# A hybrid SSD and convolution layer: another hand-written issue order for PE, DVE, ACT and POOL

## The chip, the core and the metric

The kernel runs on one core of one Trainium2 chip. The metric is the device time of one launch in microseconds (us); lower is better. The engines are named as in the profile: PE (TensorE, matmul), PEld (its weight load), DVE (VectorE), ACT (ScalarE), POOL (GpSimd), SP (SyncE, which issues all DMAs here). Each runs its own stream of instructions in order and waits on semaphores where it needs another engine's result.

## The reference, cut to what matters

One trunk layer is applied to 128 context tokens and 512 latent tokens, width 1024. All of it is float32.

```python
mod = silu(cond) @ w_ada + b_ada                # 6 shifts, scales and gates
h = rms_norm(x, norm_mix_pre) * (1 + sc1) + sh1
z, xbc, dt_raw, cf_in = split(h @ w_in)
xbc = silu(dwconv1d(xbc, w_ssd_conv))           # width 3
...
y_f, s_f = ssd_chunked(xs, dt_f, a_f, b_mat, c_mat, init_f)
y_b, s_b = ssd_chunked(flipped ...)             # 16 heads, chunks of 128 tokens
y_ssd = rms_norm((y_f + flip(y_b) + xs * d_skip) * silu(z), ssd_norm)
cf_a, cf_g = split(cf_in)
u = dwconv1d(cf_a * sigmoid(cf_g), w_cf_conv)   # width 31
u = silu(layer_norm(u))
x = x + g1 * rms_norm(concat(y_ssd, u) @ w_out, norm_mix_post)
h = rms_norm(x, norm_ffn_pre) * (1 + sc2) + sh2
up = dwconv2d(h @ w_ffn_up, w_ffn_conv)         # 3x3 on the latent grid, width 3 on context
x = x + g2 * rms_norm((silu(f_gate) * f_val) @ w_ffn_down, norm_ffn_post)
```

Outputs are the new context and latent tokens and the context's two final SSD states.

## The kernel before

**Layout.** Activations lie transposed, channels on partitions and the 640 tokens (512 latent, then 128 context) along the free side, so a vector of 1024 channels is eight tiles of 128x640. A product is split in two column halves of 384 and 256 tokens. Float32 products are made of three fp32r matmuls: each operand is split into a high part and a low rest, and `mm3` (L409, its matmul is L416) issues high x high, high x low and low x high.

**Weights.** They stream through the kernel as units of 128x1024. For each unit, SP issues the DMA into `wr` (L288, two buffers), ACT copies it rounded into `wh` (L312), POOL (for a few units DVE) makes `wl = wr - wh` (L314), and PE uses both. `wr` is free for the next DMA once `wl` is made. The names carry the unit's number: wr64, wh64, wl64.

**Stages.** From 0 to about 50 us: the adaLN products (L442, L461, transposed by L424, added to the bias by L433), the first norm and the split of the normed input (affine L535, high part L401, low rest L403). To about 375 us: the in-projection, one block of 128 channels at a time, with the SSD and the convolution of head pairs 0 to 7 woven in. To about 515 us: the out-projection, the residual and the second norm. Then up-projection with 3x3 convolution and gate, to about 850 us, down-projection, and the tail.

**The steps that the change moves, by line.**

- Width-3 convolution and SiLU of a projected block: ACT L566 (centre tap), DVE L568 and L570 (the neighbours), ACT L574 (tanh), DVE L575. L570 is the last to read the projection's PSUM bank.
- z gate: ACT L894 (tanh of the projection), DVE L895 (product, the last to read the bank).
- Width-31 convolution of one block: ACT L870 (first tap, into PSUM bank `ps2`), then up to 30 DVE taps L873 of 128x655 and the last tap in L876 and L877. Its input `u` comes from ACT L853 and DVE L858. Some far taps are made by ACT L882 and added by POOL L886.
- SSD of one head pair: `xs` is turned to tokens by PE L593 and copied by ACT L595; POOL L731 scales it; PE L745 and L747 make the chunk states in the banks `pq0` and `pq1`; ACT L749 copies these to S16 and AT or S12 and S13; POOL L757 and L760 carry the state over the chunks; ACT L790 and L797 with DVE or POOL L801 make the decay matrices S6 to S9; PE L808, DVE L810, PE L819 and DVE L824 make the output; POOL L835 and L836 and ACT L838 and L840 finish it.
- Out-projection: a product's block is squared by ACT L1078 and summed by POOL L1080 (`msq`); POOL L1159 adds the residual, ACT L1160 squares it; ACT L1179 makes the input T0, T1 ... of the up-projection, whose first products are PE L1260 (banks `ps0` and `ps1`).

**What sets the order.** The dictionary `ORDER` (from L50) holds for each of "PE", "DVE", "Activation", "Pool" and "SP" a list of indices, in the order in which the code creates that engine's instructions. `issue_in_order` (L170) chains each engine's instructions in the order of its list by dependencies without semaphores. So the list alone says what stands ahead of what on an engine; the waits between engines follow from the data.

Of the kernel before, what the change touches and what calls it, by code (L numbers as in the profile page):

```python
# [37 lines left out]
for _name, _w in (("b_ada", 48), ("g_mix_pre", 8), ("g_mix_post", 8), ("g_ffn_pre", 8),  # L38
# [24 lines left out]
1363 1450 1364-1376 1451-1460 1377-1380 1461-1466 1175-1177 1171-1174 1178 1467-1471 1381-1382 1472-1473
1383-1384 1474-1475 1385-1388 1476-1481 1389-1393 1183-1186 1179-1182 1203-1204 1394-1397 1187-1195
1205-1206 1196-1202 1398 1482-1489 1399-1402 1490-1497 1403 1498-1604 1404-1405 1408 1406-1407 1605-1641
1683 1409-1416 1684-1685 1421-1422 1417-1418 1423-1424 1419-1420 1686-1715 1441-1444 1425-1440 1731-1733
1716-1717 1734-1735 1449 1445-1448 1736-1751 1718 1752-1757 1719-1721 1642-1646 1722-1725 1758-1759 1726
1760-1773 1727-1730 1774-1778 1651-1654 1647-1650 1779-1789 1827 1790-1793 1828 1794-1795 1829-1830
1796-1826 1831 1655 1659-1662 1656-1658 1832-1869 1916 1870-1874 1679-1682 1663-1678 1917-1956 1964-1976
1957 1977 1958 1978-1984 1959-1960 1985-1987 1961 1988 1962-1963 1989-1994 1875-1879 1995-2005 2012-2018  # L70
2006 2019-2026 2007-2010 2027-2039 2011 2040-2077 1884-1885 1880-1883 1886-1905 1912-1914 1906-1908 1915
1909-1911 2078-2080 2149 2081-2107 2150-2244 2108-2112 2245-2265 2113 2266-2272 2114-2116 2357-2386
2117-2130 2387-2416 2131-2148 2417-2430 2321-2322 2431-2444 2323-2324 2273-2276 2445-2446 2317-2320
2277-2280 2447-2475 2507-2508 2476 2509-2536 2341-2344 2325-2340 2281-2292 2345-2348 2293-2296 2477-2490
2297-2308 2349-2352 2309-2312 2491-2506 2313-2316 2567-2570 2537-2541 2571-2594 2542 2595-2596 2355-2356
2353-2354 2543-2552 2597-2598 2553-2566 2599-2607 2621-2622 2608-2614 2623 2615-2620 2669-2670 2645-2646
2624 2647-2648 2625-2634 2649-2650 2635 2651-2659 2636 2660 2637-2639 2661 2640-2642 2662 2643 2663-2668
2717 2671-2672 2718-2719 2644 2673 2693-2699 2720-2722 2674-2676 2723 2700 2677-2684 2701-2707 2685-2690
2724 2708 2725 2709 2691-2692 2710-2712 2741-2744 2713-2714 2726-2729 2715 2730-2731 2745-2748 2716
2749-2750 2732 2751-2755 2733 2756 2792 2757 2734-2739 2758 2740 2759-2768 2810-2821 2769-2770 2822-2831  # L80
2771 2832-2833 2772-2778 2834-2840 2779-2782 2841 2783-2790 2894-2895 2843-2844 2791 2793-2796 2842
2797-2798 2896-2902 2799-2809 2845-2851 2903-2904 2861-2874 2852 2905-2918 2853-2860 2875 2927-2958
2876-2892 2919-2926 2960-2962 2893 2963-2966 2959 2967-2988 2993-3024 2989-2992 3026 3025 3027-3034
3092-3093 3035 3094-3098 3036-3054 3059-3090 3055-3056 3099 3057-3058 3100-3133 3203-3204 3158 3134-3137
3159 3138-3141 3160-3164 3142-3143 3165-3166 3205-3211 3144-3145 3167 3146-3147 3168 3148-3157 3169-3175
3184-3198 3176-3183 3212-3218 3301-3302 3219-3230 3236 3231-3232 3303-3306 3199-3202 3091 3307 3233
# [1511 lines left out]
```

## Time and profile before

| what | value |
|---|---|
| time before, median of 3 runs | 995.82 us (997.12, 991.63, 995.82) |
| the profiled execution's own time | 1001.64 us |
| span of its trace | 999.9 us |
| mean granted PE clock in it | 0.99 |
| bytes moved by DMA | 117.53 MB, mean 118 GB/s |
| instructions | PE 7623, DVE 1076, ACT 798, POOL 416 |

The profile shows one execution. A row of a timeline gives start and length in us, engine, line, operation, result and operands (buffer numbers left out), and in brackets the idle time just ahead of it with what ended that. A row of the chain gives start, length and what it was. In this table of 40 equal slices, each digit is the busy share of a slice in tenths, and PEclk is the clock that PE was granted:

```
PE   4899999999999999999989999999999999999995
DVE  2669988878989787541376798998988988400004
ACT  4345838667567466812454753323223236322211
POOL 0344788799987871614662896445454456543434
PEclk9999999999999999999989999999999999999997
DMA  9622534324423432589472422222222222222213
```

### The profile page before, as it was taken

To read this page: it belongs to the slowest core of one execution; us is meant where nothing else is said; L and a number is where in the kernel's file an instruction comes from. 1 tells how busy PE (TensorE), PEld (TensorE's weight loads), DVE (VectorE), ACT (ScalarE), POOL (GpSimd) and SP (SyncE) were. 2 spreads that over 40 slices of the span, in tenths; PEclk is the share of its full clock that TensorE was granted. 3 is DMA by queue.
4 is the path that set the end of the run, shared out by engine and by line. 5 is a ranking of instruction groups with operands and counts; after the bars stand their busy time and mean duration, and the time that the engine had idled before them with its cause. 6 is when DMAs were issued, how large, how long until landed. Compare 5 with 4: busy or idle time off the path is not lost.

```text
span 999.9 us, 18799 instructions
## 1 busy us (share of the span) xinstructions
PE 956.5 (96%) x7623; PEld 928.9 (93%) x7623; DVE 683.0 (68%) x1076; ACT 468.2 (47%) x798; POOL 575.3 (58%) x416
## 2 busy tenths in 40 slices
PE   4899999999999999999989999999999999999995
PEld 2799999999999888999979999999999999999995
DVE  2669988878989787541376798998988988400004
ACT  4345838667567466812454753323223236322211
POOL 0344788799987871614662896445454456543434
PEclk9999999999999999999989999999999999999997
DMA  9622534324423432589472422222222222222213
GB/s 343 252 86 66 139 89 118 117 90 144 121 84 113 124 96 72 173 284 316 143 221 64 149 85 64 85 83 66 85 75 74 85 68 71 80 80 74 80 37 106
DMA packets 50295, 117.53 MB, mean 118 GB/s; under 512 B 6016, under 2 KB 13952, under 8 KB 50208
## 3 DMA queue, kind: packets, MB, share of 16 engines
q1 hardware_dynamic: 50208, 116.33, 36.7%
q8 instruction: 60, 0.98, 0.4%
q14 instruction: 27, 0.22, 0.1%
HBM read 112.55 MB, written 3.75 MB: 116 GB/s over the span
## 4 chain that ended last, share of the span: by engine, by line
PE 73%; DMA 8%; DVE 8%; ACT 6%; POOL 4%; issue 1%; SPq 1%; POOLq 0%; ACTq 0%; DVEq 0%
PE ps L416 61%; DVE ps L873 4%; PE ps L1260 3%; DMA wr<-in_wout 3%; POOL wl L314 2%; PE pq L416 2%; DMA T<-in_wada 1%; PE pq L819 1%; ACT wh L312 1%; PE pq L808 1%; ACT S L790 1%; PE pq L461 1%; DMA wr<-in_win 1%; DMA S<-acD 1%; DMA wr<-in_wup 1%
## 5 line engine op out<-in xcount | busy, mean ns | idle before, releaser
L314 POOL TENSOR_TENSOR wl<-wr,wh 128x1024 fp32r<-128x1024 f32 (+3 forms) x127 | 290.6, 2290 | 342.2 <-ACT wh L312 309.1
L416 PE MATMUL ps<-H,wh 128*128 128x384 f32 (+1 forms) x1636 | 319.3, 310 | 3.8 <-DVE S L570 1.6
L312 ACT ACTIVATE wh<-wr 128x1024 fp32r<-128x1024 f32 (+3 forms) x131 | 131.4, 1004 | 338.7 <-PE ps L416 222.7
L416 PE MATMUL ps<-T,wh 128*128 128x384 f32 (+1 forms) x1472 | 273.3, 306 | 1.8 <-ACT S L1228 1.8
L416 PEld LDWEIGHTS ps<-H,wh 128*128 128x128 f32 x1636 | 249.5, 188 | 8.5 <-issue 4.7
L1238 DVE SCALAR_TENSOR_TENSOR S<-ps,prms,S 128x441 f32<-128x441 f32 (+2 forms) x336 | 233.4, 695 | 31.4 <-ACT S L1228 20.9
L416 PEld LDWEIGHTS ps<-T,wh 128*128 128x128 f32 x1472 | 219.5, 188 | 2.1 <-ACT S L1228 2.1
L416 PE MATMUL ps<-H,wl 128*128 128x384 f32 (+1 forms) x818 | 194.1, 310 | 1.7 <-POOL wl L314 1.7
L873 DVE SCALAR_TENSOR_TENSOR ps<-u,prms,ps 128x655 f32<-128x655 f32 x205 | 184.8, 902 | 13.0 <-ACT ps L870 8.6
L416 PE MATMUL ps<-T,wl 128*128 128x384 f32 (+1 forms) x736 | 166.8, 306 | 0.0
L416 PEld LDWEIGHTS ps<-H,wl 128*128 128x128 f32 x818 | 129.5, 188 | 3.0 <-POOL wl L314 1.9
L416 PEld LDWEIGHTS ps<-T,wl 128*128 128x128 f32 x736 | 113.0, 188 | 0.0
L489 DVE RECIPROCAL rsm<-rsm 128x160 f32<-128x160 f32 (+2 forms) x9 | 7.3, 815 | 144.9 <-ACT rsm L488 144.9
L416 PE MATMUL ps<-S,wh 128*128 128x384 f32 (+1 forms) x420 | 87.8, 311 | 0.9 <-DVE M L1073 0.8
L416 PEld LDWEIGHTS ps<-S,wh 128*128 128x128 f32 x420 | 66.6, 188 | 2.7 <-ACT wh L312 1.4
L416 PE MATMUL ps<-S,wl 128*128 128x384 f32 (+1 forms) x210 | 55.0, 310 | 1.1 <-POOL wl L314 1.0
L790 ACT ACTIVATE S<-S,AC 128x128 f32<-128x128 f32 x140 | 47.3, 394 | 14.3 <-DMA S<-acD 14.1
L886 POOL TENSOR_TENSOR T<-T,T 128x640 f32<-128x640 f32 x20 | 31.4, 1572 | 13.8 <-ACT T L882 13.8
L416 PEld LDWEIGHTS ps<-S,wl 128*128 128x128 f32 x210 | 35.3, 188 | 1.8 <-POOL wl L314 1.5
L1228 ACT ACTIVATE S<-ps,prms 128x640 f32<-128x640 f32 x42 | 36.5, 869 | 0.0
L882 ACT ACTIVATE T<-u,prms 128x512 f32<-128x512 f32 (+1 forms) x54 | 29.0, 555 | 14.4 <-POOL T L886 7.4
L1340 POOL TENSOR_TENSOR H<-S,S 128x640 f32<-128x640 f32 x16 | 25.3, 1581 | 0.0
(345 smaller groups left out, 1193.3 us busy)
## 6 DMA issues: line engine op xcount, KB each, us to landing
wr<-in_wup SPq DMA_DIRECT2D x44, 512.0 KB, 3.5
wr<-in_win SPq DMA_DIRECT2D x36, 512.0 KB, 3.7
T<-in_wada SPq DMA_DIRECT2D x49, 256.0 KB, 5.1
S<-acD SPq DMA_DIRECT2D x28, 320.0 KB, 6.0
wr<-in_wdown SPq DMA_DIRECT2D x16, 512.0 KB, 3.5
wr<-in_wout SPq DMA_DIRECT2D x13, 512.0 KB, 3.7
H<-in_wada SPq DMA_DIRECT2D x23, 256.0 KB, 5.2
S<-in_wada SPq DMA_DIRECT2D x16, 256.0 KB, 5.5
```

Of the source, the lines that this page charges most:

```text
L312: ac.activation(hi[:, :n], raw[:, :n], AF.Copy)
L314: lo_eng.tensor_tensor(lo[:, :n], raw[:, :n], hi[:, :n].bitcast(F32), SUB)
L416: last_mm[0] = te.matmul(out, w, x[:, c0:c1], start=first and i == 0, stop=last and i == 2)
L461: te.matmul(pt[32 * j:32 * j + 32, 0:P], cts[:, kc, :], w[:, j * P:(j + 1) * P], start=kc == 0, stop=kc == KD - 1, tile_position=(0, 32 * j))
L790: ac.activation(rc, rc, AF.Relu, scale=-1.0, bias=AC2[:, c, row:row + 1])
L873: ve.scalar_tensor_tensor(acc, u[:, j:j + UO], w(j), acc, MUL, ADD)
L882: ac.activation(t[:, b:c], u[:, a:a + c - b], AF.Copy, scale=w(j))
L886: gp.tensor_tensor(far, far, t, ADD)
L1228: ac.activation(out, v, AF.Identity, bias=prm_col("ffn_b", i), scale=w(1, 1))
L1238: ve.scalar_tensor_tensor(ob, vl[:, r0 + a - 1:r1 + a - 1, q0 + b - 1:q1 + b - 1], w(a, b), ob, MUL, ADD)
L1260: te.matmul(pt[:, o:o + c1 - c0], w[k] if i in (1, 2) else w[:, k * P:(k + 1) * P], x[:, c0:c1], start=k == 0 and j == 0, stop=k == KD - 1 ...
L1340: gp.tensor_tensor(f_raw[q], a, b, MUL)
```

## The change

Only the lists for "PE", "DVE", "Activation" and "Pool" in `ORDER` are written anew. "SP" and the code below the table are the same, and so is every instruction. The table is six lines shorter, so each line of the code below has a number six lower than before: L416 becomes L410, L895 becomes L889. The last index of a list that stands elsewhere belongs to work at about 540 us, so that the up-projection's loop, the down-projection and the tail come in the order of before. The start of PE's list:

```diff
     "PE": """
-0-31 36-47 32 48-50 33-34 51-67 35 68 102 69-79 103 80-100 116-120 104-105 101 106-115 121-125 140-163
+0-30 36 31 37-45 32-34 46-67 35 68-70 102 71-79 103 80-100 116-120 101 104-111 121 112-114 122-125 173-174
```

[...] Three places of it follow, with the names' numbers; the rows are of before and then of the change.

**DVE at about 312 us.** `M6_380` is the z gate of a head pair, read from the bank `ps1_379` that PE needs for its next projection; `ps2_351` is the sum of a width-31 convolution; `S0_356` is a width-3 convolution. Before:

```order
L570 SCALAR_TENSOR_TENSOR S0_356_3458<-ps0_355_3409,prms_105,S0_356_3458 128x511
L570 SCALAR_TENSOR_TENSOR S0_356_3458<-ps0_355_3409,prms_105,S0_356_3458 128x127
L873 SCALAR_TENSOR_TENSOR ps2_351_3363<-u0_111,prms_105,ps2_351_3363 128x655 x2
L824 SCALAR_TENSOR_TENSOR T4_337_3146<-S1_269_2601,prms_105,pq1_339_3165 128x128
L575 SCALAR_TENSOR_TENSOR S0_356_3458<-tanh_357_3464,S0_356_3458 128x640
L873 SCALAR_TENSOR_TENSOR ps2_351_3363<-u0_111,prms_105,ps2_351_3363 128x655 x5
L895 SCALAR_TENSOR_TENSOR M6_380_3640<-M6_380_3640,ps1_379_3591 128x640
L873 SCALAR_TENSOR_TENSOR ps2_351_3363<-u0_111,prms_105,ps2_351_3363 128x655 x8
```

and now:

```order
L564 SCALAR_TENSOR_TENSOR S0_356_3458<-ps0_355_3409,prms_105,S0_356_3458 128x511
L564 SCALAR_TENSOR_TENSOR S0_356_3458<-ps0_355_3409,prms_105,S0_356_3458 128x127
L867 SCALAR_TENSOR_TENSOR ps2_351_3363<-u0_111,prms_105,ps2_351_3363 128x655
L818 SCALAR_TENSOR_TENSOR T4_337_3146<-S1_269_2601,prms_105,pq1_339_3165 128x128
L867 SCALAR_TENSOR_TENSOR ps2_351_3363<-u0_111,prms_105,ps2_351_3363 128x655 x3
L569 SCALAR_TENSOR_TENSOR S0_356_3458<-tanh_357_3464,S0_356_3458 128x640
L867 SCALAR_TENSOR_TENSOR ps2_351_3363<-u0_111,prms_105,ps2_351_3363 128x655 x4
L889 SCALAR_TENSOR_TENSOR M6_380_3640<-M6_380_3640,ps1_379_3591 128x640
L867 SCALAR_TENSOR_TENSOR ps2_351_3363<-u0_111,prms_105,ps2_351_3363 128x655 x9
```

Counted from the start of DVE's list, two convolution taps fewer stand ahead of the z gate; nine instead of eight follow it.

**ACT at about 326 us.** `S16_365` and `AT_367` are the copies of the chunk states out of the banks `pq0_364` and `pq1_366`, which PE needs for L808; `T4_337` is a finished SSD output; `ps2_390` is the start of the next width-31 convolution; wh34 to wh36 are weight copies. Before:

```order
L312 ACTIVATE wh34_3721<-wr34_3719 128x1024
L853 ACTIVATE u1_115<-ps0_388_3668 128x128
L797 ACTIVATE S6_343_3235<-S6_343_3235,EB_710 128x640
L774 ACTIVATE S10_347_3243<-S10_347_3243 128x512
L312 ACTIVATE wh35_3812<-wr35_3810 128x1024
L840 ACTIVATE T4_337_3146<-T4_337_3146,prms_105 128x640
L870 ACTIVATE ps2_390_3776<-u1_115,prms_105 128x655
L749 ACTIVATE S16_365_3518<-pq0_364_3513 128x512
L749 ACTIVATE AT_367_3526<-pq1_366_3521 128x512
L312 ACTIVATE wh36_3992<-wr36_3990 128x640
```

and now:

```order
L306 ACTIVATE wh34_3721<-wr34_3719 128x1024
L791 ACTIVATE S6_343_3235<-S6_343_3235,EB_710 128x640
L306 ACTIVATE wh35_3812<-wr35_3810 128x1024
L743 ACTIVATE S16_365_3518<-pq0_364_3513 128x512
L743 ACTIVATE AT_367_3526<-pq1_366_3521 128x512
L864 ACTIVATE ps2_390_3776<-u1_115,prms_105 128x655
L560 ACTIVATE S1_393_3865<-ps0_392_3816,prms_105 128x640
L784 ACTIVATE S6_382_3648<-S6_382_3648,AC2_715 128x128
L306 ACTIVATE wh36_3992<-wr36_3990 128x640
```

The two state copies stand ahead of the convolution's first tap now, and the scaling of `T4_337` has moved behind them, out of these rows.

**POOL at about 500 us.** wl62 to wl65 are low rests of weight units; `M5_578` and `M2_539` are blocks of the residual sum, `msq` the sum of squares. Before:

```order
L314 TENSOR_TENSOR wl62_5700<-wr62_5696,wh62_5698 128x1024
L1159 TENSOR_TENSOR M5_578_5418<-M5_578_5418,T13_575_5367 128x384
L1159 TENSOR_TENSOR M2_539_5109<-M2_539_5109,T10_572_5361 128x384
L314 TENSOR_TENSOR wl63_5715<-wr63_5711,wh63_5713 128x384
L1080 TENSOR_TENSOR msq_4894<-msq_4894,S16_593_5692 128x256
L314 TENSOR_TENSOR wl64_5795<-wr64_5791,wh64_5793 128x1024
L1080 TENSOR_TENSOR msq_4894<-msq_4894,S17_597_5778 128x256
```

and now:

```order
L308 TENSOR_TENSOR wl62_5700<-wr62_5696,wh62_5698 128x1024
L308 TENSOR_TENSOR wl63_5715<-wr63_5711,wh63_5713 128x384
L1153 TENSOR_TENSOR M2_539_5109<-M2_539_5109,T10_572_5361 128x384
L1153 TENSOR_TENSOR M5_578_5418<-M5_578_5418,T13_575_5367 128x384
L1074 TENSOR_TENSOR msq_4894<-msq_4894,S16_593_5692 128x256
L1074 TENSOR_TENSOR msq_4894<-msq_4894,S17_597_5778 128x256
L308 TENSOR_TENSOR wl64_5795<-wr64_5791,wh64_5793 128x1024
```

wl63 has moved ahead of the two residual sums, and wl64 behind the second sum of squares. On PE, the first two units of the up-projection (wh65 and wh66) are used three products of the one, then the other before; now it is ten of the one, up to its fourth channel block, before the first of the other.

Elsewhere in the lists steps of the same kinds change places by a few positions. On PE, the transposes L593 of one head pair at about 132 us follow directly on the products L745 and L747 where 26 projection products stood between them. On DVE, at about 224 us, one more tap L873 stands ahead of the two products L810. On ACT, in the first 25 us, the copy L401 of the second channel block stands behind the first two weight copies.

More of the change, by code (lines that the diff above doesn't have):

```diff
@@ new lines @@
+2293-2296 2477-2490 2297-2304 2349-2352 2305-2312 2491-2506 2313-2316 2567-2569 2537-2544 2570-2573
+2545-2549 2574-2593 2597-2598 2594-2596 2550-2566 2599-2612 2621-2623 2355-2356 2353-2354 2613-2620 2669
+2624-2626 2645 2627-2628 2670 2629-2635 2646-2651 2636-2637 2652-2664 2638-2644 2693-2702 2671-2678
+2665-2666 2703-2704 2667 2679-2690 2668 2717-2722 2705-2706 2691-2692 2707-2710 2723-2729 2711-2716
+2741-2742 2730-2737 2743-2749 2738-2740 2750-2755 2792 2756-2769 2810-2812 2770 2813-2828 2771-2777
@@ new lines @@
+6669-6676""",
+    "DVE": """
+0-2 13-14 3 15-16 4-5 18-19 6-8 17 9 20 11-12 23-24 28 25 29 26 10 30 27 21-22 33-36 38-40 37 31-32 41-42 46
+43-44 47 45 48-50 84 51-52 85 53-54 86-90 111-112 91 113 55-56 114 92 69 57-61 119-122 93-99 62 100-102
+63-66 124 67 125 68 103 70-71 75 104-107 72-73 108-110 76-77 123 78-83 126 152 127 153-155 128-129 163
+130-131 74 115 117 132-133 156 116 118 158 134-142 164-165 143-144 193-196 157 145-151 166-170 160 159 171
+204 161-162 197 172-183 205 184-185 206 186-190 199 198 191 234-236 192 237 200-201 207-211 238-239 212-213
@@ new lines @@
+589-590 592-596 598 601-602 599-600 605 603-604 606-612 615-616 613-614 617-749 1053 750-1046 1049-1051
+1047-1048 1052 1054-1063 1065 1064 1066-1075""",
+    "Activation": """
+0-3 5 4 7 6 8-10 15 18 11-12 19 17 21-22 20 24 13 25 23 27 26 35 32 28-29 14 16 33 48 47 30 56 61 57 49-50
+34 51 62-63 52-53 64-66 31 58 54-55 71 67 79 37-46 36 59 68 80 60 116 120 117 86-88 81 69-70 91 72 92-94 89
+73-74 101-104 96 105 113 75-76 123 121-122 77-78 97 109 98-99 82-83 100 112 95 111 90 110 133 108 134 84-85
@@ new lines @@
+688 686 690 687 689 693 691 695 692 694 698 696 700 697 699 703 701 727 705 702 704 708 706 709 707 714
+710-713 715 719 716 725-726 717 720 731 718 723 721-722 732 724 728-729 733-734 730 735 741 736-740 745
+742-744 746-747 751 748-750 752-753 757 754-756 758-759 763 760-762 764-765 769 766-768 770-771 775 772-774
+776-784""",
+    "Pool": """
+0-13 16-19 14-15 24-25 20-21 26 22 27 33 65 23 69 28-30 36 70 35 34 51 75 31 37-38 48 39-41 49 42-45 50
+46-47 52 93 97 64 53 32 54-61 71 66-67 77 76 62-63 98 103 80-82 72 79 83 78 104 73-74 84 92 99 105 68 85-86
@@ L159 @@
+396-397 399 398 400-411""",
     "SP": """
```

179 lines of the change are left out of this document (75 added, 104 removed).

## The prediction

> **What bounds the kernel now.** I read the page first, then busy time by stretch, then PE's own timeline for every place where it stood idle.
>
> ```profile
> PE 956.5 (96%) x7623; PEld 928.9 (93%) x7623; DVE 683.0 (68%) x1076; ACT 468.2 (47%) x798; POOL 575.3 (58%) x416
> PE 73%; DMA 8%; DVE 8%; ACT 6%; POOL 4%; issue 1%; SPq 1%; POOLq 0%; ACTq 0%; DVEq 0%
> ```
>
> ```profile
> 0.00:50.00 50.00, 34.22 (x445) 24.94 (x446) 22.09 (x49) 20.05 (x30) 9.84 (x22) 1.00 0.82 298
> 125.00:575.00 450.00, 432.50 (x3710) 415.57 (x3709) 329.49 (x499) 266.44 (x499) 308.67 (x258) 0.99 0.44 140
> 575.00:975.00 400.00, 400.00 (x2819) 399.58 (x2818) 257.42 (x405) 130.51 (x168) 203.86 (x104) 1.00 0.25 74
> ```
>
> The first two lines are the page's busy time by engine and the chain that ended last. The next three give, for one stretch each, its length and the busy time of PE, PEld, DVE, ACT and POOL, then PE's granted clock, the DMA share and GB/s. PE is busy 956.5 of 999.9 us and carries 73% of the chain; 575 to 975 us holds no idle time at all. A new order adds and removes no instruction, so it can only touch PE's idle time and PE's clock: 15.8 us of idle in the first 50 us, 17.5 between 125 and 575, and the clock there. From about 545 us on the order is as it was, and so is what PE loses there.
>
> These are ten stops of PE between 125 and 350 us, each put to another engine (start, length, engine, line, form, and in brackets the idle time ahead with its releaser):
>
> ```profile
> 141.04 0.94 PE L745 MATMUL pq<-S,M 128*128 128x128 f32 x6 [0.41 <-POOL S L731]
> 195.33 0.83 PE L416 MATMUL ps<-H,wh 128*128 128x384 f32 x4 [0.94 <-DVE S L570]
> 231.74 0.54 PE L416 MATMUL ps<-H,wh 128*128 128x384 f32 x2 [0.34 <-DVE S L570]
> 256.59 0.60 PE L808 MATMUL pq<-M,S 128*128 128x128 f32 x3 [0.47 <-ACT AT L749]
> 265.50 0.83 PE L416 MATMUL ps<-H,wh 128*128 128x384 f32 x4 [0.22 <-DVE M L570]
> 278.95 0.56 PE L416 MATMUL ps<-H,wh 128*128 128x384 f32 x2 [0.43 <-DVE S L895]
> 281.15 0.45 PE L416 MATMUL ps<-H,wh 128*128 128x384 f32 x1 [0.27 <-ACT u L853]
> 312.79 0.45 PE L416 MATMUL ps<-H,wh 128*128 128x384 f32 x1 [1.28 <-DVE M L895]
> 327.20 0.53 PE L808 MATMUL pq<-M,st 128*128 128x128 f32 x2 [2.01 <-ACT S L749]
> 344.98 0.83 PE L416 MATMUL ps<-H,wh 128*128 128x384 f32 x4 [0.35 <-DVE S L570]
> ```
>
> In all of them PE needs a result, or a PSUM bank, that a short step on DVE, ACT or POOL gives free, and that step stood behind work nobody was waiting for. This is what an order can mend.
>
> **A stop can also cost clock.**
>
> ```profile
> 312.00:316.00 4.00, 3.21 (x22) 3.21 (x23) 3.89 (x6) 4.00 (x14) 3.70 (x4) 1.00 0.41 128
> 328.00:332.00 4.00, 4.00 (x35) 3.77 (x36) 1.94 (x3) 0.00 (x0) 1.30 (x3) 0.63 0.15 38
> 516.00:520.00 4.00, 4.00 (x20) 3.40 (x19) 1.94 (x4) 2.22 (x5) 1.82 (x1) 0.50 0.96 318
> ```
>
> After the stop of 1.28 us at 312.79 the clock stays at 1.00. Behind the 2.01 at 327.20 it is 0.63 for 4 us, a loss of 0.37 x 4 = 1.48 us. Behind the stop at 515.44 (row below) it is 0.50: 0.50 x 4 = 2.00 us. So here a stop of about 2 us costs clock, and one of 1.3 doesn't.
>
> [...]
>
> **The change, part by part.** The sum is made against the profiled execution, 1001.64 us, which lies 5.82 above the median of the runs, 995.82.
>
> *1. Ten stops that go: -6.72.* In all ten rows the step waited for stands earlier than it did, against the PE work behind it. At 312.79, the DVE and ACT rows of before are these:
>
> ```profile
> L873 DVE SCALAR_TENSOR_TENSOR ps<-u,prms,ps 128x655 f32<-128x655 f32 x162 | 146.1, 902 | 10.2 <-ACT ps L870 6.6
> 310.24 0.68 ACT L894 ACTIVATE M<-ps 128x640 f32<-128x640 f32 x1
> 311.92 0.81 DVE L895 SCALAR_TENSOR_TENSOR M<-M,ps 128x640 f32<-128x640 f32 x1
> ```
>
> Two taps of L873 leave the front of L895: 2 x 0.90 = 1.80 us, more than the stop of 1.28. Its input from ACT (L894) would hold it at 310.92, but L894 is also moved ahead of the weight copy that stood in front of it, so both follow. At 327.20:
>
> ```profile
> 325.73 0.90 ACT L870 ACTIVATE ps<-u,prms 128x655 f32<-128x655 f32 x1 [3.13 <-DVE u L858]
> 326.57 0.58 ACT L749 ACTIVATE S<-pq 128x512 f32<-128x512 f32 x1
> ```
>
> ACT had idled 3.13 us at L870 while PE's state products lay finished in PSUM; their copy L749 now stands ahead of L870 and of L840. The others are alike: L570 has two taps fewer ahead at 195.33 and 231.74 (1.8 us) and four fewer at 265.50 and 344.98 (3.6), L895 one at 278.95 (0.9); the copies L749 at 256.59 and L853 at 281.15 and the POOL step L731 at 141.04 are 1.1 to 4.4 us of work earlier. Each of these exceeds its stop. The ten add up to 0.41 + 0.94 + 0.34 + 0.47 + 0.22 + 0.43 + 0.27 + 1.28 + 2.01 + 0.35 = 6.72. What is late next is PE itself. The bounds are 0 and -6.72.
>
> *2. The clock behind 327.20: -1.48*, as above, bounds 0 and -1.48.
>
> *3. New stops: +2.74.* PE's xs transposes L593, which stood 26 products behind the state products, now follow them at once, and they write the bank that the copy L749 empties:
>
> ```profile
> 128.90 0.66 PE L416 MATMUL ps<-H,wh 128*128 128x256 f32 x3
> 129.44 0.59 ACT L749 ACTIVATE S<-pq 128x512 f32<-128x512 f32 x1
> 224.01 0.69 DVE L810 TENSOR_TENSOR S<-S,pq 128x512 f32<-128x512 f32 x1 [0.48 <-PE pq L808]
> ```
>
> PE was through with the products at 128.90, and the copy ends at 130.03: a stop of about 1.0 (the copy itself is moved little). Behind PE there waits the whole in-projection; nothing else waits on L593 soon. At 224.01 DVE gets one tap more (0.90) ahead of L810, of which 0.48 was idle: 0.4 for L819 on PE. I add two stops of the mean size of the ten, 2 x 0.67 = 1.34, for places that come to light only when several engines move at once. The other stop in this stretch, at L808 near 172 us, I leave as it is: its products and their copy move forward together. Bounds 0 and 4.8, the latter if seven of mean size arise.
>
> *4. The first 50 us: -0.5.*
>
> ```profile
> 22.52 0.74 ACT L401 ACTIVATE H<-T 128x640 fp32r<-128x640 f32 x1 [3.71 <-DVE T L535]
> 25.17 2.15 DVE L403 TENSOR_TENSOR H<-T,H 128x640 fp32r<-128x640 f32 x1 [0.80 <-ACT H L401]
> 29.59 0.44 PE L416 MATMUL ps<-H,wl 128*128 128x384 f32 x1 [1.65 <-POOL wl L314]
> ```
>
> The copy for the second channel block (0.74) leaves the front of the first two weight copies, so the pair of wl steps for which PE waits 1.65 us starts earlier; the DVE steps L403 fall beside them still. I take two thirds of 0.74. Bounds: -1.65 (the whole wait) and +2.15 (one more L403 of this length in front of PE).
>
> *5. Around 500 to 516 us: +0.5.* Here the chain runs on a weight unit's DMA, its copy, its wl step, and the next DMA into the buffer that wl frees.
>
> ```profile
> 507.79 0.71 POOL L1080 TENSOR_TENSOR msq<-msq,S 128x256 f32<-128x256 f32 x1
> 507.85 6.46 DMA wr<-in_wup
> 510.38 0.62 ACT L1179 ACTIVATE T<-HL,modv 128x384 fp32r<-128x384 f32 x1 [1.64 <-DVE HL L1177]
> 512.59 0.52 PE L1260 MATMUL ps<-T,wh 128*128 128x384 f32 x2
> 512.94 0.34 PE L1260 MATMUL ps<-T,wl 128*128 128x384 f32 x1
> 515.30 0.40 ACT L1078 ACTIVATE S<-M 128x256 f32<-128x256 f32 x1
> 515.44 1.01 PE L1260 MATMUL ps<-T,wh 128*128 128x384 f32 x2 [2.16 <-ACT wh L312]
> ```
>
> The second msq step (0.71) now stands ahead of wl64, so the wup transfer behind it starts 0.71 later. PE has seven more products of the first unit ahead of the late one, (512.94 - 512.59) / 2 = 0.175 each, 1.2 in all; but the seventh needs the fourth channel block, whose copy stands behind wh66 and L1078 on ACT: 0.40 + 0.62. That is 0.71 + 1.02 - 1.2 = 0.5. SP's order is untouched; its next DMA waits for wl64 either way. Bounds: -4.2 (rival C) and +1.7 (the seven hide nothing).
>
> Sum: -6.72 - 1.48 + 2.74 - 0.5 + 0.5 = **-5.46**; 996.18 on the profiled execution's own time, and 995.82 - 5.46 = **990.4** by the median.
>
> **The rivals.**
>
> *A, DVE gives it back: 995.3.* A producer is earlier only because taps are later, and the taps end in results that PE needs too.
>
> ```profile
> 275.00:300.00 25.00, 24.30 (x195) 23.43 (x194) 21.03 (x28) 17.31 (x34) 21.40 (x19) 1.00 0.27 84
> 300.00:325.00 25.00, 23.72 (x170) 23.44 (x168) 24.18 (x28) 18.52 (x41) 19.50 (x14) 1.00 0.34 113
> ```
>
> DVE is busy 24.18 of 25 us from 300 to 325. Then the six stops on DVE's lines come back elsewhere (0.94 + 0.34 + 0.22 + 0.43 + 1.28 + 0.35 = 3.56) with two more of mean size (1.34): 990.4 + 4.9. Against it: DVE idles 3.97 us in the stretch ahead.
>
> *B, slower: 1001.9.* DVE takes its steps in order, so a producer that is moved ahead of its own input stops the taps behind it.
>
> ```profile
> 352.59 0.82 DVE L895 SCALAR_TENSOR_TENSOR S<-S,ps 128x640 f32<-128x640 f32 x1 [1.63 <-ACT S L894]
> ```
>
> If the six DVE steps moved forward each wait 1.63 us for ACT, as here, DVE gets 9.78 us longer. Its idle time from 275 to 325 takes 3.97 + 0.82 = 4.79 of that; 4.99 is left for PE, the six stops stay (3.56), and two of them grow beyond 2 us (0.94 + 1.63 and 1.28 + 1.63) and cost clock, 2 x 1.48. That is 990.4 + 4.99 + 3.56 + 2.96. It decides from three such steps on (4.89 against 4.79). Against it speaks that L894 is moved forward along with L895.
>
> *C, better than forecast: 986.2.* The wup transfer that took 6.46 us is slow for its kind:
>
> ```profile
> wr<-in_wup SPq DMA_DIRECT2D x44, 512.0 KB, 3.5
> ```
>
> At the usual 3.5 the stop of 2.16 and the 2.00 us of clock behind it would go: -4.2. For it: other engines reach this place at other times. Against it: the queue ahead of it is the same.
>
> **How the numbers follow.** The forecast has a chance of 0.46, spread over some 986.5 to 994; A 0.33; B 0.13; C 0.08. A measurement of this kernel can tell about 0.5% from no change, 5.0 us: below 990.8 is faster, above 1000.8 slower. Six tenths of the forecast lie below 990.8, 0.28, and with C that is 0.36 for faster; the rest of it and A give 0.51 for no change; B gives 0.13. The range goes from 985.0 (the forecast without the new stops, -2.7, and with the whole start-up wait gone, -1.2, is 986.5; C is 986.2, and some of both lies lower) to 1000.0, which is A with the bounds of the new stops (+2.1) and of the start-up (+2.6) on top, and leaves out B.
>
> **What would show it.** Right, if PE's rows in the trace after show no stop ahead of the products that follow L895 and L749 at about 312 and 327 us, and a granted clock of 1.00 there; idle time between 125 and 575 us of 11 to 13 us in place of 17.5; a stop of about 1 us at L593 near 132; and 515 us still with its stop and its half clock. Wrong, if PE's idle time there is 17 us with other lines as releasers (A), if DVE's L895 or L570 are themselves idle for ACT (B), or if the clock is 1.00 from 515 us on (C). A change in the stretch beyond 575 us would be against all of it.

## The result, and the profile after

The change takes 990.35 us (median of 16 runs, 988.39 to 993.91) where before takes 996.03 (16 runs, 991.63 to 1000.85). The ratio is 0.9948, with a 95% interval of 0.9933 to 0.9963: 5.2 us faster; 5.46 were forecast. The profiled execution of the change took 988.39 us. That of before took 1001.64, more than any of its 16 timed runs, so the two traces lie 13.3 us apart and their medians 5.7. Of the 13.3, 6.2 are idle time of PE (35.2 us in all before, 29.0 after), 4.0 are products at a slower pace, of which the last section tells, and about 1 is the mean granted clock (0.990 before, 0.991 after); the other 2 us are not assigned. What that means for single terms is seen below.

The page and busy time by stretch of the change (length, busy time of PE, PEld, DVE, ACT, POOL, then PE's clock, the DMA share and GB/s):

```profile
PE 949.5 (96%) x7623; PEld 922.6 (94%) x7623; DVE 688.6 (70%) x1076; ACT 469.9 (48%) x798; POOL 574.2 (58%) x416
PE 80%; DMA 6%; DVE 4%; ACT 4%; POOL 3%; issue 2%; SPq 0%; POOLq 0%; ACTq 0%; DVEq 0%
```

```profile
0.00:50.00 50.00, 37.18 (x455) 28.51 (x456) 24.97 (x49) 20.34 (x31) 10.31 (x22) 0.93 0.82 298
50.00:125.00 75.00, 72.65 (x511) 72.03 (x510) 63.66 (x101) 46.46 (x91) 39.60 (x21) 1.00 0.33 97
125.00:575.00 450.00, 438.12 (x3791) 421.76 (x3790) 342.42 (x518) 275.61 (x510) 320.46 (x266) 1.00 0.44 142
```

PE's share of the chain rises from 73 to 80%, and its idle time between 125 and 575 us falls from 17.5 to 11.9 us. But 2.35 us of idle time stand between 50 and 125, where there was none. These are PE's stops in the change that matter here, in order of time:

```profile
96.56 0.61 PE L659 MATMUL pq<-csts,T 128*32 128x128 f32 x4 [2.35 <-DVE T L630]
130.19 0.82 PE L587 MATMUL pq<-csts,S 128*128 128x128 f32 x5 [0.69 <-ACT S L743]
206.85 0.44 PE L410 MATMUL ps<-H,wh 128*128 128x384 f32 x1 [0.33 <-ACT u L847]
253.00 0.57 PE L802 MATMUL pq<-M,S 128*128 128x128 f32 x3 [0.37 <-ACT AT L743]
318.91 0.49 PE L802 MATMUL pq<-M,st 128*128 128x128 f32 x2 [0.24 <-ACT S L743]
505.53 0.44 PE L1254 MATMUL ps<-T,wh 128*128 128x384 f32 x1 [0.36 <-ACT T L1173]
511.23 1.03 PE L455 MATMUL pq<-S,cts 128*32 128x128 f32 x29 [1.34 <-DMA S<-in_wada]
549.01 0.75 PE L410 MATMUL ps<-T,wh 128*128 128x384 f32 x3 [1.77 <-ACT S L1222]
```

Of the ten stops, eight are gone and two are left with 0.37 (was 0.47) and 0.24 us (was 2.01). The stop near 172 us is gone too. The one at L587 (L593 before) is new, as forecast. The stop at 515 us, 2.16 us before, is 0.36, and a new one of 1.34 us waits for a transfer shortly after it.

### The profile page after: what moved, and what is told of

Read it like the earlier page. It is cut to its first block, busy times and chain, and to the rows that moved or that the text cites. A ratio compares the mean times of both kernels' runs of the same rounds, so it can differ in the third digit from the quotient of the medians.

```text
span 986.6 us, 18794 instructions
## 1 busy us (share of the span) xinstructions
PE 949.5 (96%) x7623; PEld 922.6 (94%) x7623; DVE 688.6 (70%) x1076; ACT 469.9 (48%) x798; POOL 574.2 (58%) x416
## 4 chain that ended last, share of the span: by engine, by line
PE 80%; DMA 6%; DVE 4%; ACT 4%; POOL 3%; issue 2%; SPq 0%; POOLq 0%; ACTq 0%; DVEq 0%
PE ps L410 68%; DMA wr<-in_wout 2%; PE pq L410 2%; PE ps L1254 2%; PE pq L813 2%; DVE ps L867 1%; DMA T<-in_wada 1%; PE pq L802 1%; POOL wl L308 1%; PE pq L455 1%; PE pq L739 1%; DMA wr<-in_wup 1%; PE pq L436 1%; ACT wh L306 1%; DMA S<-in_wada 1%
## 5 line engine op out<-in xcount | busy, mean ns | idle before, releaser
L410 PE MATMUL ps<-H,wh 128*128 128x384 f32 (+1 forms) x1636 | 315.8, 309 | 0.3 <-ACT u L847 0.3
L410 PE MATMUL ps<-T,wh 128*128 128x384 f32 (+1 forms) x1472 | 273.0, 306 | 1.8 <-ACT S L1222 1.8
L410 PEld LDWEIGHTS ps<-H,wh 128*128 128x128 f32 x1636 | 247.7, 188 | 3.3 <-issue 2.5
L410 PEld LDWEIGHTS ps<-T,wh 128*128 128x128 f32 x1472 | 219.6, 188 | 2.2 <-ACT S L1222 2.1
L410 PE MATMUL ps<-H,wl 128*128 128x384 f32 (+1 forms) x818 | 190.8, 308 | 0.0
L410 PE MATMUL ps<-T,wl 128*128 128x384 f32 (+1 forms) x736 | 166.6, 306 | 0.0
L410 PEld LDWEIGHTS ps<-H,wl 128*128 128x128 f32 x818 | 128.6, 188 | 0.5 <-issue 0.4
L410 PEld LDWEIGHTS ps<-T,wl 128*128 128x128 f32 x736 | 113.3, 188 | 0.0
L410 PE MATMUL ps<-S,wh 128*128 128x256 f32 (+1 forms) x420 | 88.1, 310 | 0.9 <-ACT wh L306 0.4
L410 PEld LDWEIGHTS ps<-S,wh 128*128 128x128 f32 x420 | 66.5, 188 | 2.1 <-issue 0.8
L410 PE MATMUL ps<-S,wl 128*128 128x384 f32 (+1 forms) x210 | 55.0, 311 | 1.0 <-DVE wl L308 0.6
L410 PEld LDWEIGHTS ps<-S,wl 128*128 128x128 f32 x210 | 35.1, 188 | 2.3 <-DVE wl L308 0.9
L795 POOL TENSOR_TENSOR S<-S,M 128x640 f32<-128x640 f32 x14 | 22.0, 1574 | 8.8 <-ACT S L791 8.8
```

The source lines that it names most:

```text
L410: last_mm[0] = te.matmul(out, w, x[:, c0:c1], start=first and i == 0, stop=last and i == 2)
L795: (ve if i % 2 or last else gp).tensor_tensor(r, r, cbm[g][d], MUL)
```

## The experiments

The first seven kernels and the last mix the two tables. A stretch "from a to b us" holds, on all four engines, the instructions that started in it in the trace of before; inside a stretch they stand in the order of the one table or of the other. Ratios are against before, run on the same chip; they are not the quotients of the medians given here, and the verdicts go by them.

**The change up to 125 us.** ACT in the first 25 us is a typical piece:

```diff
+L401 ACTIVATE H0_60_360<-T0_1_71 128x640
+L312 ACTIVATE wh0_188<-wr0_186 128x1024
+L312 ACTIVATE wh1_194<-wr1_192 128x1024
 L401 ACTIVATE H1_62_366<-T1_2_73 128x640
-L312 ACTIVATE wh0_188<-wr0_186 128x1024
-L401 ACTIVATE H0_60_360<-T0_1_71 128x640
-L312 ACTIVATE wh1_194<-wr1_192 128x1024
```

> Order of the change up to 125 us, order of before from there on. The two traces differ by +0.6 us at 125 us: a gain of 3.6 by 50 us and a new stop of 2.35 us at about 96 us that gives it back. Theory (the gain comes from the stops between 125 and 375 us): 0 to +1 us against before, ratio 0.999 to 1.002. Rival (the gain comes from the start): 2 to 4 us faster, ratio 0.996 to 0.998.

Measured: 998.11 us, ratio 1.0025 (1.0003 to 1.0047), 2.5 us slower. The interval excludes the rival: the start carries no gain. The stop at L665 is there, 2.35 us, as in the change.

**The change from 125 to 375 us.**

```diff
-L873 SCALAR_TENSOR_TENSOR ps2_351_3363<-u0_111,prms_105,ps2_351_3363 128x655 x5
+L873 SCALAR_TENSOR_TENSOR ps2_351_3363<-u0_111,prms_105,ps2_351_3363 128x655 x4
 L895 SCALAR_TENSOR_TENSOR M6_380_3640<-M6_380_3640,ps1_379_3591 128x640
```

> Order of the change from 125 to 375 us, order of before ahead of it and behind it. Theory: the ten stops and their clock less two or three new stops, 5 to 8 us faster, ratio 0.992 to 0.995, and a trace without the stops at 312 and 327 us. Rival (DVE gives it back, or the gain comes from elsewhere): within 1.5 us of before, ratio 0.9985 to 1.001.

Measured: 988.92 us, ratio 0.9937 (0.9920 to 0.9954), 6.3 us faster. This stretch carries the gain. By the ratios it is about 1 us more than the whole change brings, but the two intervals overlap.

**The change from 375 us on.**

```diff
+L314 TENSOR_TENSOR wl63_5715<-wr63_5711,wh63_5713 128x384
 L1159 TENSOR_TENSOR M2_539_5109<-M2_539_5109,T10_572_5361 128x384
-L314 TENSOR_TENSOR wl63_5715<-wr63_5711,wh63_5713 128x384
```

> Order of before up to 375 us, order of the change from there on. Theory (term +0.5): within 1 us of before, ratio 0.999 to 1.001. Rival (the stop at 515 us and its half clock go): 3 to 4 us faster, ratio 0.996 to 0.997.

Measured: 996.64 us, ratio 1.0011 (0.9994 to 1.0029). No difference can be told; a gain of 3 us is excluded. Up to 375 us this kernel has the order of before, and its trace is a second look at that order:

```profile
172.70 0.91 PE L808 MATMUL pq<-M,S 128*128 128x128 f32 x6 [1.03 <-ACT AT L749]
311.71 0.76 PE L416 MATMUL ps<-H,wh 128*128 128x384 f32 x4
325.58 0.49 PE L808 MATMUL pq<-M,st 128*128 128x128 f32 x2 [0.59 <-ACT S L749]
```

There is no stop at the 312-us place, and 0.59 in place of 2.01 us at the 327-us one, with the clock at 1.00. The kernel with the change up to 125 us has the order of before in this stretch too; its trace has no stop at the 312-us place and 0.24 us at the other. So the two largest of the ten stops come and go from one execution to the next. Where they come from is seen on DVE and POOL, first in before, then in the kernel with the change from 375 us on:

```profile
305.19 1.57 POOL L836 TENSOR_TENSOR T<-T,S 128x640 f32<-128x640 f32 x1 [0.59 <-DVE T L824]
305.27 2.17 DVE L575 SCALAR_TENSOR_TENSOR S<-tanh,S 128x640 f32<-128x640 f32 x1 [0.23 <-ACT tanh L574]
```

```profile
306.15 0.83 DVE L575 SCALAR_TENSOR_TENSOR S<-tanh,S 128x640 f32<-128x640 f32 x1
306.20 2.20 POOL L836 TENSOR_TENSOR T<-T,S 128x640 f32<-128x640 f32 x1 [0.83 <-DVE T L824]
```

The one that started first, by 0.08 us there and by 0.05 here, ran at its own pace (1.57 us for L836, 0.83 for L575), and the other one took longer by nearly what was left of the first: in before DVE loses 1.34 of the 1.49 us that POOL's step still had, in the other trace POOL loses 0.63 of 0.78. In before DVE was the loser, and L895 and L749 behind it came late. What the two steps contend for, the traces don't show.

**The order of before up to 125 us, the change from there on.** The edit is the sum of the two before it, and the pieces shown there are in it.

> Order of before up to 125 us, order of the change from there on; so the new stop at 96 us isn't made, nor is what the change gains in the first 50 us. Theory: as fast as the change or up to 1 us faster, ratio to before 0.993 to 0.995. Rival (the start carries the gain): 2 to 4 us slower than the change, ratio 0.997 to 0.999.

Measured: 986.74 us, ratio 0.9928 (0.9903 to 0.9953), 7.2 us faster than before; the change itself is 5.2 faster. The rival is excluded.

**The change from 285 to 345 us alone**, with the two largest stops in it. ACT's piece, without what stands between:

```diff
+L749 ACTIVATE S16_365_3518<-pq0_364_3513 128x512
+L749 ACTIVATE AT_367_3526<-pq1_366_3521 128x512
 L870 ACTIVATE ps2_390_3776<-u1_115,prms_105 128x655
-L749 ACTIVATE S16_365_3518<-pq0_364_3513 128x512
-L749 ACTIVATE AT_367_3526<-pq1_366_3521 128x512
```

> Order of the change from 285 to 345 us alone; it mends the stops at 312.79 and 327.20 us. Theory of the prediction: 1.28 + 2.01 + 1.48 of clock = 4.8 us faster, ratio 0.995. Rival (these stops belong to one execution: POOL L836 started 0.08 us ahead of DVE L575, which then took 2.17 in place of 0.83 us, and two traces with the same order there have no stop at 312 and 0.59 us or less at 327): 0.5 to 2.5 us faster, ratio 0.9975 to 0.9995.

Measured: 995.28 us, ratio 0.9995 (0.9978 to 1.0013). The 4.8 us of the prediction are excluded. The trace has no stop at the 312-us place and 0.24 us at the 327-us one.

**The change from 125 to 285 us alone.** DVE at its start:

```diff
-L873 SCALAR_TENSOR_TENSOR ps2_112_1048<-u1_115,prms_105,ps2_112_1048 128x655 x5
+L873 SCALAR_TENSOR_TENSOR ps2_112_1048<-u1_115,prms_105,ps2_112_1048 128x655 x2
+L801 TENSOR_TENSOR S9_125_1167<-S9_125_1167,M1_104_858 128x640
+L873 SCALAR_TENSOR_TENSOR ps2_112_1048<-u1_115,prms_105,ps2_112_1048 128x655
 L568 SCALAR_TENSOR_TENSOR T15_183_1637<-ps0_182_1588,prms_105,T15_183_1637 128x511
```

> Order of the change from 125 to 285 us alone. Theory of the prediction: stops of 0.41 + 0.94 + 0.34 + 0.47 + 0.22 + 0.43 + 0.27 = 3.08 us go and 1.4 to 2.1 come, 1 to 1.7 us faster, ratio 0.998 to 0.999. Rival (the stop of 1.40 us near 172, which was left as it is, goes too, and the new ones are smaller): 3 to 5 us faster, ratio 0.995 to 0.997.

Measured: 995.32 us, ratio 0.9995 (0.9976 to 1.0014). The rival is excluded. The interval still holds the 1 to 1.7 us of the theory, and no change as well. The trace shows a gain that is given back:

```profile
293.61 0.66 PE L819 MATMUL pq<-S,S 128*64 128x128 f32 x8 [1.52 <-POOL S L801]
310.44 0.73 PE L416 MATMUL ps<-H,wh 128*128 128x384 f32 x3 [0.87 <-DVE M L895]
324.86 0.66 PE L808 MATMUL pq<-M,st 128*128 128x128 f32 x2 [2.02 <-ACT S L749]
```

```profile
286.85 4.79 POOL L314 TENSOR_TENSOR wl<-wr,wh 128x1024 fp32r<-128x1024 f32 x2
292.01 1.54 POOL L801 TENSOR_TENSOR S<-S,M 128x640 f32<-128x640 f32 x1
```

PE comes earlier to the old order of 285 to 345 us and finds POOL's L801 behind two wl steps, and then both known stops. The tie at 305 us was lost here too: POOL's L836 starts at 302.84, DVE's L575 at 303.26, and L575 takes 1.83 us. So some of what is given back may be this one execution's; only the times of the 12 runs say that it is no exception.

**The change from 125 to 345 us**, so both halves at once.

> Order of the change from 125 to 345 us, so both halves that brought 0.5 us each when alone, without 345 to 375. Theory (one half alone is given back: what the first saves is lost to port ties and waits in the old order of the second, and the second alone mends what only some executions lose): 5 to 7 us faster, ratio 0.993 to 0.995. Rival (the gain of 125 to 375 us lies in 345 to 375): about 1 us, ratio 0.998 to 1.000.

Measured: 989.09 us, ratio 0.9936 (0.9911 to 0.9961), 6.4 us faster, where neither half alone can be told from no change (0.5 us each by the ratios) and 345 to 375 adds nothing that can be told. Of what the theory calls port ties the traces show only that a DVE or a POOL step took longer beside one of the other engine, here L575 1.83 in place of 0.83 us in the trace with 125 to 285 us alone; that a port is behind it, no run shows. With three PE rows as marks (the first L745 after 125 us, the second L819 of head pair 4 near 262 us, the first L474 near 350 us; in the change they are L739, L813 and L468), the traces give these times between marks, each the difference of two start times:

| order in 125 to 285, in 285 to 345 | traces | L745 to L819, us (idle in it) | L819 to L474, us (idle in it) |
|---|---|---|---|
| before, before | 3 | 135.4 to 135.7 (3.1 to 3.6) | 86.0, 87.1, 90.6 (1.5, 3.2, 5.1) |
| change, before | 1 | 131.8 (1.4) | 89.5 (4.8) |
| before, change | 1 | 134.6 (3.6) | 86.6 (2.0) |
| change, change | 7 | 131.6 to 132.7 (1.5 to 2.0) | 83.7 to 84.5 (0.7 to 1.2) |

The three of the old order are before and the kernels with the change up to 125 and from 375 us on; the seven are the change and all kernels with its order from 125 to 345. The thirteenth trace, that of the next experiment, is not counted. The new order of the first stretch saves some 3 us in the first column, about half of it idle time (the other half is met again behind the experiments). In the second column the old order varies by 4.6 us from one execution to the next, the new one by 0.8, and 84 us stand only where both stretches are new. The two mixed orders have one trace each, but what they show goes with the times.

**The tie at 305 us decided by order.** Two neighbours on DVE change places:

```diff
+L575 SCALAR_TENSOR_TENSOR S0_356_3458<-tanh_357_3464,S0_356_3458 128x640
 L824 SCALAR_TENSOR_TENSOR T4_337_3146<-S1_269_2601,prms_105,pq1_339_3165 128x128
-L575 SCALAR_TENSOR_TENSOR S0_356_3458<-tanh_357_3464,S0_356_3458 128x640
```

> Before, with two neighbours on DVE changed over: L575 now stands ahead of L824 of T4_337, which releases POOL's L836; so L836 can't start ahead of L575. Theory (a tie lost in some executions makes the stops at 312 and 327 us): L575 at its 0.83 us, no stop over 1 us at 312 and 327, and 0.5 to 2.5 us faster by the median, ratio 0.9975 to 0.9995. Rival (the tie is of no account): ratio 1.000, within 0.001.

Measured: 994.30 us, ratio 0.9998 (0.9982 to 1.0014). L575 takes 0.82 us, there is no stop at 312 us and 0.58 at 327, as the theory says. Of the five traces with the old order here, the two in which POOL started first (before, and the change from 125 to 285 us alone) have the stops, 0.87 us and more at both places; the three in which DVE did have none at 312 and at most 0.59 us at 327. But in the times nothing is to be seen (a gain above 1.8 us is excluded), so the tie isn't lost often enough to matter much, or is paid for elsewhere. Nor does the change avoid the collision: its L575 takes 1.96 us in the trace of the change, only PE doesn't wait for it.

**The new stop at 96 us.** In the change, on POOL and DVE:

```profile
90.04 2.51 POOL L308 TENSOR_TENSOR wl<-wr,wh 128x1024 fp32r<-128x1024 f32 x1 [3.70 <-ACT wh L306]
90.18 2.46 DVE L637 TENSOR_SCALAR T<-T 128x160 f32<-128x160 f32 x1
92.56 3.71 DVE L867 SCALAR_TENSOR_TENSOR ps<-u,prms,ps 128x655 f32<-128x655 f32 x4
96.19 0.32 DVE L630 COPY T<-pq 128x160 f32<-128x160 f32 x1
```

L637 (L643 in the other numbering) has one input and takes 0.23 or 0.24 us in the traces where no POOL step runs beside it. Here POOL started 0.14 us ahead, and L637 ended 0.09 us after the wl step did. First it was moved behind, here against the change and with the line numbers of before:

```diff
 L627 SCALAR_TENSOR_TENSOR T9_84_673<-T12_85_677,aexp_692 128x160
-L643 TENSOR_SCALAR T9_84_673<-T12_85_677 128x160
-L873 SCALAR_TENSOR_TENSOR ps2_91_737<-u0_111,prms_105,ps2_91_737 128x655 x4
+L873 SCALAR_TENSOR_TENSOR ps2_91_737<-u0_111,prms_105,ps2_91_737 128x655 x2
 L636 COPY T13_87_699<-pq1_86_695 128x2x5x16
 L639 TENSOR_TENSOR WD_701<-pq1_86_695,T13_87_699 128x160
+L873 SCALAR_TENSOR_TENSOR ps2_91_737<-u0_111,prms_105,ps2_91_737 128x655 x2
+L643 TENSOR_SCALAR T9_84_673<-T12_85_677 128x160
```

> The change, with DVE's one-input step L643 (L637 in the change) moved from behind L627 to behind four convolution taps, L636 and L639, and L636 and L639 two taps earlier. In the change L643 took 2.46 in place of 0.24 us beside a POOL step that had started 0.14 us before it, and PE stopped 2.35 us for L636. Theory (the stop at 96 us is this lock): no stop there, L643 below 1 us, and 2 to 2.5 us faster than the change, ratio to before 0.992 to 0.993. Rival (PE would wait for L636 anyway, or the gain is lost by the next bound): as the change, ratio 0.9945 to 0.9955.

Measured: 993.05 us, ratio 0.9979 (0.9963 to 0.9995). Both expectations missed: it is about 3 us slower than the change.

```profile
94.48 0.61 PE L665 MATMUL pq<-csts,T 128*32 128x128 f32 x4 [0.42 <-DVE T L636]
99.19 0.39 PE L665 MATMUL pq<-csts,T 128*32 128x128 f32 x1 [2.97 <-ACT CDs L659]
```

```profile
96.71 0.34 ACT L644 ACTIVATE T<-T 128x160 f32<-128x160 f32 x1 [4.65 <-DVE T L643]
97.06 1.28 ACT L645 ACT_TABLE_LOAD   x1
98.60 0.54 ACT L659 ACTIVATE CDs<-pq 128x16 f32<-128x16 f32 x6
```

The stop for L636 is down to 0.42, but ACT stands 4.65 us at L644 for the late L643, and L659, which frees the bank that PE needs, is queued behind it and a table load. Behind the stop of 2.97 us the granted clock is 0.86 and 0.71 in the two windows of 4 us from 96 to 104 us, 1.7 us of clock in sum, where the change has 1.00 in both. Stops of 3.39 in place of 2.35 us and this clock make 2.8 us, about what the times show. L643 takes 0.24 us again, and a longer wait stands in the place of the stop. So L643 was then moved ahead instead:

```diff
-L873 SCALAR_TENSOR_TENSOR ps2_91_737<-u0_111,prms_105,ps2_91_737 128x655
 L624 SCALAR_TENSOR_TENSOR T12_85_677<-T9_84_673 128x160
 L627 SCALAR_TENSOR_TENSOR T9_84_673<-T12_85_677,aexp_692 128x160
 L643 TENSOR_SCALAR T9_84_673<-T12_85_677 128x160
-L873 SCALAR_TENSOR_TENSOR ps2_91_737<-u0_111,prms_105,ps2_91_737 128x655 x4
+L873 SCALAR_TENSOR_TENSOR ps2_91_737<-u0_111,prms_105,ps2_91_737 128x655 x5
```

> The change, with the DVE tap that stands ahead of L624 put behind L643 instead: L643 runs 0.8 us earlier, ahead of the POOL step that locked it out. Theory: L643 at 0.24 us, the stop for L636 at about 0.3 in place of 2.35 us, 2 us faster than the change, ratio to before 0.992 to 0.9935. Rival (another step is late there, as when L643 was put behind): no faster than the change, ratio 0.9945 to 0.998.

Measured: 987.99 us, ratio 0.9925 (0.9901 to 0.9950), 2.3 us below the change by the ratios, as the theory says, though the two intervals just overlap. Against the attempt before, with L643 behind, they don't.

```profile
89.61 0.24 DVE L643 TENSOR_SCALAR T<-T 128x160 f32<-128x160 f32 x1
94.36 0.32 DVE L636 COPY T<-pq 128x160 f32<-128x160 f32 x1
94.74 0.50 PE L665 MATMUL pq<-csts,T 128*32 128x128 f32 x3 [0.42 <-DVE T L636]
```

**The change up to 50 us and from 125 us on, before in between.** The edit leaves the new lists without their piece from 50 to 125 us.

> Order of the change up to 50 us, of before from 50 to 125, of the change from there on. Theory (what the change gains at the start, 2.0 us at 90 us in the traces, lasts where the lock at 96 us isn't made): 1 to 3 us faster than with the order of before up to 125 us, ratio to before 0.990 to 0.9915. Rival (the first weight units set the pace there and the start gains nothing that lasts): as with the order of before up to 125, ratio 0.9925 to 0.995.

Measured: 987.18 us, ratio 0.9917 (0.9888 to 0.9946). This lies between the two expectations, and the interval holds both; whether the first 50 us gain anything stays open. This kernel, the one with L643 moved ahead and the one with the change from 125 us on are 7 to 8 us faster than before. They can't be told apart. By their medians all three are below the change, but each interval overlaps the change's.

## Why the prediction was right, and where it wasn't

The forecast of 990.4 us meets the 990.35 measured, and the place was right: 125 to 375 us alone brings 6.3 us, the terms forecast for it come to -6.72 - 1.48 + 2.74 = -5.46. The reason was right for the larger part: PE had waited for short steps that stood behind work nobody needed yet, and these waits went. That the number is met this closely is luck. Stops and clock were priced too high from one slow execution, and a part of the gain that the prediction ruled out made up for it.

- *Ten stops that go, -6.72.* Eight of the ten are gone and the two others are smaller. The sizes were those of one execution that was slower than any timed run. In the trace of the kernel that differs from before only behind 375 us, they add up to 4.25 us (0.41, 0.94, 0.34, 0.52, 0.21, 0.57, 0.32, 0.59 and 0.35, none at 312). For the stop at 278.95 the reading was wrong: L895 there had itself been idle 1.91 us for ACT's L894, so a tap fewer ahead of it could not by itself mend it. The test of the two largest alone brought 0.5 us, not 1.28 + 2.01 + 1.48.
- *The clock behind 327.20, -1.48.* It too belongs to some executions: the trace with the stop of 0.59 has a clock of 1.00 there, and the kernel with the change from 125 to 285 us alone has 0.63 there, behind a stop of 2.02. The prediction took what one trace showed as a rule. Where the clock does fall, the term was read too small: over the windows on both sides as well, the rows of before give 0.06 x 4 + 0.37 x 4 = 1.72 us from 324 to 332, and 3.40 us, not 2.00, from 512 to 524.
- *The stop near 172 us, left as it is.* Wrong. It is 1.40, 1.03 and 0.69 us in the three traces of the old order and gone in the new. Both sides moved forward, but the copy more than the products: they end at 162.45 in place of 169.55 us, and the later copy starts at 162.49 in place of 171.09.
- *New stops, +2.74.* At L593 0.69 us, forecast 1.0; at L819 0.14, forecast 0.4. The two of 1.34 in sum that were added without a place turned out as 0.19 near 145, 0.33 near 207 and 2.35 us at 96 us, the last of these outside the stretch that I had searched. What failed there is the view: the rows of before hold no idle time between 50 and 125 us, so I priced no step there, and a step of 0.24 us that took 2.46 beside a POOL step wasn't looked for.
- *The first 50 us, -0.5.* With the stop at 96 us in it the part up to 125 us costs 2.5 us; without it, the gain is not told from none. The clock of 0.93 up to 50 us in the trace of the change isn't its order's: ten of the 13 traces, of either order, lose clock there, and before is one of the three that don't.
- *500 to 516 us, +0.5.* The sum holds within its error (1.1 us slower for all from 375 us on, interval -0.6 to 2.9). The mechanism doesn't: I expected the stop and its half clock to stay. The stop is 0.36 us, the clock 1.00, and 1.34 us is lost at the next transfer instead. The order is not what decides this: the seven traces with the old order there have a stop of 0.34 to 2.42 us, and of these only before has a lower clock behind it.
- *Rival C, the usual transfer of 3.5 us.* Its sign, a clock of 1.00 from 515 us on, came true, and its gain of 4.2 us didn't: the change from 375 us on alone gains 0.6 us at most. The sign didn't tell the cases apart, because what it was to remove was for the most part one execution's. Nor was the transfer odd: the one in this place takes 3.9 to 6.7 us in the 13 traces.
- *Rival A, DVE gives it back.* It didn't come about for the change as a whole, but its kind of mechanism did where only 125 to 285 us was changed: in its one trace, POOL and ACT more than DVE gave the gain back.
- *Rival B, slower.* No trace of the new order shows a wait of L895 or L570 for ACT in front of a stop of PE. The order of before has one, at 278 us (1.91 us for L894), and it is gone. What did cost time was one kind of head-of-line wait that I had put on DVE and that the first attempt at a repair made on ACT.
- *What the sum left out.* The prediction held that an order can touch only PE's idle time and its clock. It also changed the time that PE is busy with the same products. The rows are of the kernel with the change from 375 us on, which has the old order here, and of the change, from the first mark of the table to the last:

```profile
128.05:350.67 222.62, 216.15 (x1651) 210.65 (x1650) 191.49 (x256) 148.28 (x297) 193.81 (x175) 1.00 0.39 116
127.56:343.15 215.59, 212.81 (x1652) 208.87 (x1650) 193.12 (x256) 146.25 (x293) 194.32 (x176) 1.00 0.38 118
```

Of the 7.0 us between them, 3.7 are idle time and 3.3 busy time. Over the three traces of the old order and the seven of the new one it is 7.1 us in the mean: 3.8 idle time, 0.6 clock (before alone) and 2.7 busy time. About 1 of the 2.7 is the slower pace of products (last section): between 125 and 375 us it takes 2.9 to 3.7 us in the three traces and 1.3 to 2.7 in the seven. For the rest one sees that PE changes between L416 and other products 54 times in the old order and 40 times in the new; that this is the cause was not tried, and no run separates it from the stops.

Put together with these sizes, an estimate from single traces, 125 to 375 us gives -4.25 for the ten stops, +0.61 for the two that are left, -1.03 for the one near 172, +1.35 for the new ones and -2.7 for busy time: -6.0, where 6.3 us was measured.

That the halves need each other was shown by the times, and the traces go with it; which of the moves in 285 to 345 us lets the gain through was not tried.

## What to carry to other kernels

Before you price a stop from one trace, look whether that execution is a typical one: here it stood above all timed runs, and its two largest stops were small or absent in two other traces of the same order. An order can also change how long an engine is busy with the same work, so compare busy time as well as stops. A stop that an order makes is also a matter of the stretch behind: a gain ahead of a tight stretch shows only when that stretch is mended too, so test stretches together as well as alone. And when a short step on DVE stands near a long one on POOL, put it ahead with a margin (here 0.14 us behind cost 2.2 us, and 0.54 us ahead cost nothing), and check whose queue stands behind it before you move it back.

## What the runs showed of the hardware that was not expected

- **A DVE step with a single SBUF input took ten times as long beside a POOL step**: 2.46 in place of 0.24 us for a TENSOR_SCALAR of 128x160 with the POOL step started 0.14 us before it, in the two traces in which they met (the change, and the kernel with the change up to 125 us). What makes it wait, the traces don't show.
- **The clock after a stop is not decided by its length alone.** The stop near 550 us is the same work in every kernel, 1.76 or 1.77 us; the rows below are of before and then of the change, at the same place:

```profile
560.00:564.00 4.00, 3.08 (x21) 3.11 (x22) 3.77 (x8) 4.00 (x7) 4.00 (x4) 1.00 0.98 354
564.00:568.00 4.00, 4.00 (x29) 4.00 (x28) 3.82 (x8) 3.97 (x7) 3.92 (x5) 1.00 0.44 145
```

```profile
548.00:552.00 4.00, 2.99 (x13) 3.02 (x14) 3.77 (x8) 4.00 (x7) 4.00 (x4) 0.69 0.96 356
552.00:556.00 4.00, 4.00 (x26) 4.00 (x26) 3.82 (x8) 3.97 (x7) 3.92 (x5) 0.88 0.43 138
```

Of the 13 traces, three show a lower clock behind it, ten don't: 0.69 and 0.88 in the change as above, and in the windows from 552 to 560 us 0.81 and 0.76 where the tie was decided by order, 0.61 and 0.97 where L643 was moved behind. The other way round, the change's stop of 2.35 us at 96 us has 1.00 behind it, as the row of 50 to 125 us shows. So the prediction's reading, that a stop of about 2 us costs clock and one of 1.3 doesn't, is no rule for when the clock falls. What decides it, no run here shows.

- **The same products ran at two paces under one granted clock.** PE's rows in the trace of before, six products of 384 and 256 columns in turn from one wl row to the next:

```profile
610.19 0.46 PE L416 MATMUL ps<-T,wl 128*128 128x384 f32 x2
610.49 0.76 PE L416 MATMUL ps<-T,wh 128*128 128x384 f32 x4
611.09 0.46 PE L416 MATMUL ps<-T,wl 128*128 128x384 f32 x2
611.48 1.96 PE L461 MATMUL pq<-H,cts 128*32 128x128 f32 x64
613.36 0.85 PE L416 MATMUL ps<-T,wh 128*128 128x384 f32 x4
614.05 0.45 PE L416 MATMUL ps<-T,wl 128*128 128x384 f32 x2
614.34 0.73 PE L416 MATMUL ps<-T,wh 128*128 128x384 f32 x4
614.91 0.45 PE L416 MATMUL ps<-T,wl 128*128 128x384 f32 x2
```

The six take 0.90 us (610.19 to 611.09) ahead of the L461 products and 0.86 (614.05 to 614.91) behind them, with no idle time in either and a granted clock of 1.00 in both (609 to 611.5 and 613.3 to 615.2 us). Added up over the product line, the slower pace costs 7.1 us in the trace of before and 3.1 in that of the change. Behind 500 us it costs 2.2 us in six of the 13 traces and at most 0.2 in the other seven, with tails of either table in both groups, so this part goes with the execution and not with the order. What sets the pace was not tried.
